# A convolution with max pooling: the GpSimd block of each step regrouped and placed behind the sums of the next step

## Chip, cores, metric

The kernel runs on one core of one Trainium2 chip. The metric is the device time of one execution in microseconds (us); the kernel before was run 13 times, and the median counts.

## What is computed

A 3x3 convolution (stride 1, padding 1, no bias) of 16 images with 64 channels of 64x64 points to 128 channels, and then the maximum over 2x2 points. All inputs and outputs are fp32.

```python
x_pad = np.pad(x, ((0, 0), (0, 0), (pad, pad), (pad, pad)), mode='constant')
conv[b, co] += weight[co, ci, kh, kw] * x_pad[b, ci, kh:kh+h, kw:kw+w]
...
output[b, c, i, j] = np.max(conv[b, c, i*pool_size:(i+1)*pool_size,
                                      j*pool_size:(j+1)*pool_size])
```

## The kernel before

**Tiling.** Two images of 64 channels fill the 128 partitions, so the 16 images are 8 pairs. Each pair is cut into 4 parts of 8 output rows (16 image rows). The 32 parts are worked through in 16 steps, i = 0 to 15, i = 4j + q. Step i does part q of two pairs: an even one, called "k" (tile kx, loaded as bf16), and an odd one, called "w" (tile wx, loaded as fp32).

**Fewer products.** The convolution's two rows under one output row share work. Call the four image rows concerned x(-1), x0, x1, x2, and the filter's rows g0, g1, g2. For "k", PA forms (g2 - g1) x1 + g0 x(-1) in one accumulator, PB forms (g0 - g1) x0 + g2 x2 in a second. The row maximum is taken (MX), and g1 (x0 + x1), which both rows have in common, is added to the result afterwards (PR). For "w", P2 forms half of (g0 + g2 - g1) times x1 - x0 in one accumulator, ScalarE writes its negative to a second (SE); P0 adds g0 (x(-1) - x1) to the first and P3 adds g2 (x2 - x0) to the second; after the maximum (mx), P1 adds half of (g0 + g1 + g2) times x0 + x1. PA and PB have 12 matmuls each, the other five have 6 each: 54 matmuls in a step.

**Row operations.** The sums and differences of image rows are made ahead of the matmuls, each as one `tensor_tensor` over 128x512 elements (`row_op`, line 244):

| name in the order | tile | what | engine | read by |
|---|---|---|---|---|
| KS | ks | x0 + x1 of "k" | VectorE | PR |
| WS | ws | x0 + x1 of "w" | VectorE | P1 |
| E | we | x1 - x0 of "w" | VectorE up to step 4, GpSimd from step 5 | P2 |
| Z | wz | x(-1) - x1 of "w" | GpSimd | P0 |
| Y | wy | x2 - x0 of "w" | GpSimd | P3 |

**The rest of a step.** ScalarE copies one accumulator to SBUF (EV, ev), VectorE takes the row maximum with the other (MX, mx: `rowmax`, line 297), ScalarE copies the odd columns (OD, od), and VectorE takes the column maximum of the even columns with them (CM, cm: `colmax`, line 313). That result goes to tile o and is stored by SyncE's queue. There are four accumulators and four o buffers; CM and cm give an accumulator back, and need an o buffer whose store has landed.

**Loads.** `wload` brings the part of the "w" pair for step i + 4 and is issued by SyncE behind the store of CM.i. `kload` brings half of the next "k" pair; GpSimd issues it inside `wy` (line 269), after the Y of the parts q = 1 and q = 2.

**Order.** The order on every engine is written out by hand (`tc.manual_schedule()`): HEAD for steps 0 to 3, STEADY for steps 4 to 12 ("Z+1" in step i means Z of step i + 1), TAIL for the rest. Each engine takes its own steps out of this list in order. Apart from the waits for data there is one that the kernel adds: each GpSimd row operation waits for the last VectorE row operation written ahead of it in the list. `on_vector` (line 74) notes it, `on_gpsimd` (line 78) adds the wait:

```python
def on_gpsimd(inst):
    behind(inst, sbuf_op[0])
    return inst
```

In STEADY, E+1, Z+1 and Y+1 are written in the first half of step i, so the last VectorE row operation ahead of them is WS.i, at the end of step i - 1.

Of the kernel before, what the change touches and what calls it, by code (L numbers as in the profile page):

```python
# [11 lines left out]
def kernel(  # L12
# [265 lines left out]
    ev, od, ot = {}, {}, {}  # L278
# [91 lines left out]
    for m in BLOCKS:  # L370
# [6 lines left out]
        P0.0 P3.0 Z.1 Y.1 OD.0 CM.0 P2.1 ev.0 PB.1 SE.1 mx.0 P0.1 P1.0 MX.1 P3.1 ev.1 od.0 PR.1  # L377
        WS.2 KS.2 E.2 Z.2 Y.2 OD.1 cm.0 CM.1 PA.2 EV.2 P2.2 PB.2 SE.2 mx.1 P1.1 P0.2 MX.2 P3.2
        od.1 ev.2 cm.1 E.3 KS.3 WS.3 Z.3 Y.3 PR.2 PA.3 OD.2 CM.2 P2.3 mx.2 EV.3 PB.3 SE.3 P1.2
        MX.3 P0.3 od.2 P3.3 cm.2 ev.3 PR.3 E.4 KS.4 WS.4 Z.4 Y.4  # L380
    """
    STEADY = """
        PA+0 OD-1 E+1 CM-1 P2+0 mx-1 EV+0 Z+1 PB+0 SE+0 Y+1 P1-1 MX+0 P0+0 od-1 P3+0 cm-1 ev+0
        PR+0 KS+1 WS+1
    """
    TAIL = """
        PA.13 OD.12 CM.12 Y.14 P2.13 mx.12 EV.13 PB.13 SE.13 P1.12 KS.14 MX.13 E.14 P0.13 od.12
        P3.13 cm.12 ev.13 KS.15 PR.13 WS.14 OD.13 PA.14 EV.14 CM.13 mx.13 P2.14 SE.14 PB.14
        MX.14 P1.13 od.13 cm.13 Z.14 P0.14 ev.14 E.15 WS.15 PR.14 OD.14 CM.14 PA.15 P2.15 P3.14
        mx.14 Y.15 Z.15 EV.15.0 EV.15.1 PB.15 MX.15.1 MX.15.0 SE.15 P0.15 P3.15 ev.15.0 mx.15.0  # L390
        ev.15.1 mx.15.1 P1.14 od.14 cm.14 PR.15 OD.15 CM.15 P1.15 od.15 cm.15
    """
    FIRST, LAST = 4, 12
# [53 lines left out]
```

## Time and profile before

| | |
|---|---|
| median of 13 executions | 108.91 us |
| lowest and highest | 108.51 and 110.9 us |
| the profiled execution's own time | 110.9 us |
| its span | 109.1 us |
| TensorE busy | 99.9 us, 900 matmuls |
| VectorE busy | 84.6 us |
| ScalarE busy | 72.9 us |
| GpSimd busy | 60.1 us |
| Z, Y and E on GpSimd | 16, 16 and 11 instructions, mean 1271, 1281 and 1272 ns |
| KS and WS on VectorE | 16 and 16 instructions, mean 468 and 841 ns |
| kx loads by GpSimd's queue | 7, about 0.5 MB written each, 5.9 to 10.5 us to landing |

The profile is of one execution, and its span is what the engines' records cover; the difference of 1.8 us to the execution's time lies around it. A line of the timeline gives the start and the duration in us, the engine, the line in the kernel, the tile written and the tiles read with their shapes, and how often; a bracket gives the engine's idle time before it and what ended it. Line 248 is that of all row operations, so the tile's name tells which one it is. Line 183 is that of all matmuls of the convolution. A matmul's end is modelled, so the length of a group of matmuls is best taken from the start of one group to the start of the next.

### The profile page before, as it was taken

Reading aid. Unit: us, or ns where it says so; the run is one execution under the profiler, and the core shown is the slowest. Engines: PE = TensorE matmul, PEld = TensorE weight load, DVE = VectorE, ACT = ScalarE, POOL = GpSimd, SP = SyncE. Lnnn points to the kernel's source line nnn. Section 1 sums busy time; section 2 is a strip of 40 time slices with the busy share of each in tenths; the row PEclk is TensorE's granted clock in tenths of the full one; section 3 lists DMA queues with packets and bytes.
Section 4 is the critical chain, followed back from the end, with each engine's and each line's share of the span. In section 5 each row is a group of like instructions: output and inputs, shape, how many; then the busy total and the mean of one; then the engine's idle time right before and its main releaser. Section 6 shows DMA issues by size and latency. Waiting matters only on the chain.

```text
span 109.1 us, 2346 instructions
## 1 busy us (share of the span) xinstructions
PE 99.9 (92%) x900; PEld 50.1 (46%) x900; DVE 84.6 (77%) x113; ACT 72.9 (67%) x92; POOL 60.1 (55%) x69
## 2 busy tenths in 40 slices
PE   5999989999999969999999999959999999999820
PEld 2564434444444435555555555525555555545400
DVE  0498989879797989688787868639787888685950
ACT  4568965776867656776867676764867676776820
POOL 6205673915439997948578594904967444535000
PEclk9999999999999999999999999999999999999998
DMA  3999966999978469999948789996939422223052
GB/s 95 325 338 346 262 169 151 204 292 257 297 278 205 176 62 199 296 203 392 262 160 225 107 169 244 224 304 249 265 137 207 165 102 99 96 96 102 0 192 97
DMA packets 12475, 21.96 MB, mean 201 GB/s; under 512 B 944, under 2 KB 9136, under 8 KB 12464
## 3 DMA queue, kind: packets, MB, share of 16 engines
q1 hardware_dynamic: 11312, 18.03, 50.3%
q0 software_dynamic: 1008, 3.65, 21.5%
q8 instruction: 7, 0.11, 0.4%
q10 hardware_dynamic: 144, 0.13, 0.3%
q14 instruction: 4, 0.03, 0.1%
HBM read 17.07 MB, written 8.39 MB: 233 GB/s over the span
## 4 chain that ended last, share of the span: by engine, by line
PE 61%; DMA 17%; DVE 14%; issue 3%; ACT 2%; DVEq 0%
PE acc L183 59%; DMA out_dram<-o 12%; DVE acc L299 6%; DMA wx<-in_x_dram 5%; DVE ws L248 4%; DVE o L318 2%; PE acc L135 2%; ACT od L304 2%; DVE ks L248 2%; DVE we L248 1%; DVE zeros L112 0%; DVE wt L163 0%; DVEq L299 0%; DVEq L318 0%
## 5 line engine op out<-in xcount | busy, mean ns | idle before, releaser
L183 PEld LDWEIGHTS <-wt 64*128 64x128 bf16 x864 | 46.7, 94 | 49.9 <-issue 4.1
L183 PE MATMUL acc<-kx,wt 64*128 64x504 bf16 (+3 forms) x384 | 46.5, 373 | 2.3 <-DVE o L318 2.3
L299 DVE TENSOR_TENSOR acc<-acc,ev 128x1024 f32<-128x1024 f32 (+1 forms) x34 | 39.5, 1165 | 11.5 <-PE acc L183 10.8
L286 ACT COPY ev<-acc 128x1024 f32<-128x1024 f32 (+1 forms) x34 | 32.5, 963 | 14.0 <-PE acc L183 10.2
L304 ACT COPY od<-acc 128x512 f32<-128x512 f32 x32 | 18.8, 587 | 12.7 <-PE acc L183 12.6
L248 POOL TENSOR_TENSOR wz<-wx 128x512 bf16<-128x512 f32 x16 | 20.3, 1271 | 12.5 <-DVE ws L248 5.7
L318 DVE TENSOR_TENSOR o<-acc,od 128x512 f32<-128x512 f32 x32 | 21.9, 689 | 5.0 <-ACT od L304 3.2
L248 POOL TENSOR_TENSOR wy<-wx 128x512 bf16<-128x512 f32 x16 | 20.5, 1281 | 5.0 <-DVE ws L248 5.0
L248 POOL TENSOR_TENSOR we<-wx 128x512 bf16<-128x512 f32 x11 | 14.0, 1272 | 15.0 <-DVE ws L248 9.1
L295 ACT ACTIVATE acc<-acc 128x1024 f32<-128x1024 f32 x16 | 16.1, 1008 | 1.4 <-PE acc L183 1.0
L183 PE MATMUL acc<-ws,wt 64*128 64x504 bf16 (+1 forms) x96 | 13.2, 377 | 0.4 <-DVE acc L299 0.4
L183 PE MATMUL acc<-we,wt 64*128 64x504 bf16 (+1 forms) x96 | 13.2, 377 | 0.4 <-DVE we L248 0.4
L248 DVE TENSOR_TENSOR ws<-wx 128x512 bf16<-128x512 f32 x16 | 13.4, 841 | 0.0
L183 PE MATMUL acc<-ks,wt 64*128 64x504 bf16 (+1 forms) x96 | 13.2, 377 | 0.1
L183 PE MATMUL acc<-wz,wt 64*128 64x504 bf16 (+1 forms) x96 | 13.2, 377 | 0.0
L183 PE MATMUL acc<-wy,wt 64*128 64x504 bf16 (+1 forms) x96 | 13.2, 377 | 0.0
L248 DVE TENSOR_TENSOR ks<-kx 128x512 bf16<-128x512 bf16 x16 | 7.5, 468 | 0.0
L95 POOL DMA_DIRECT2D kx<-in_x_dram x7 | 4.2, 594 | 4.1 <-DVE we L248 4.1
L135 PE MATMUL acc<-zeros 128*128 128x512 bf16 x8 | 3.6, 631 | 1.2 <-DVE zeros L112 1.2
L248 DVE TENSOR_TENSOR we<-wx 128x512 bf16<-128x512 f32 x5 | 3.4, 684 | 0.4 <-DMA wx<-in_x_dram 0.4
L148 PEld LDWEIGHTS <-wq 128*128 128x128 bf16 x28 | 2.3, 124 | 1.0 <-issue 0.6
L148 PE MATMUL acc<-ident,wq 128*128 128x128 bf16 x28 | 2.6, 264 | 0.0
(26 smaller groups left out, 14.9 us busy)
## 6 DMA issues: line engine op xcount, KB each, us to landing
out_dram<-o SPq DMA_DIRECT2D x31, 256.0 KB, 3.7
wx<-in_x_dram SPq DMA_DIRECT2D x8, 512.0 KB, 6.0
wx<-in_x_dram SPq DMA_DIRECT2D x4, 544.0 KB, 6.9
kx<-in_x_dram POOLq DMA_DIRECT2D x4, 496.0 KB, 8.5
wx<-in_x_dram SPq DMA_DIRECT2D x4, 480.0 KB, 4.8
kx<-in_x_dram POOLq DMA_DIRECT2D x3, 528.0 KB, 7.6
kfirst<-in_x_dram SPq DMA_DIRECT2D x1, 544.0 KB, 4.2
ksecond<-in_x_dram SPq DMA_DIRECT2D x1, 512.0 KB, 6.3
```

Of the source, the lines that this page charges most:

```text
L95: return nc.gpsimd.dma_start(out=kx[j][:, lo:hi, :], in_=rows_of(2 * j, lo, hi))
L135: return nc.tensor.matmul(acc[t][:, h], zeros[:, 0:128], zeros, start=True, stop=True, skip_group_check=True)
L148: nc.tensor.transpose(tp[:, (j - lo) * 128 : (j - lo + 1) * 128], wq[:, j : j + 2, :].rearrange("a b c -> a (b c)"), ident,)
L183: nc.tensor.matmul(dst[:, half, i0:i1, o0:o1], wt[lo : lo + CI, m0 + kw - half, :], rows(lo, i0, i1, c0, c1), start=start and kw == 1, sto ...
L248: return engine.tensor_tensor(out=row_out(name, i), in0=row_in(t, f + a, pad), in1=row_in(t, f + b, pad), op=op)
L286: nc.scalar.copy(out=ev[g][:, halves(h)], in_=acc[ta[g]][:, halves(h)])
L295: nc.scalar.mul(acc[t], acc[ta["w", i]], -1.0)
L299: nc.vector.tensor_tensor(out=t, in0=t, in1=ev[g][:, halves(h)], op=MAX)
L304: nc.scalar.copy(out=od[g][:, halves(h)], in_=acc[tb[g]][:, halves(h), :, 1::2])
L318: nc.vector.tensor_tensor(out=o, in0=acc[tb[g]][:, s, :, 0::2], in1=od[g][:, s], op=MAX)
```

## The change

The three GpSimd row operations of a step stay three, but the group is put together differently and written elsewhere in the list. Before, it is E, Z, Y of step i + 1, spread over the first half of step i. After, it is Z and Y of step i + 1 and E of step i + 2, written at the end of step i, behind KS+1 and WS+1. With `on_gpsimd` unchanged, its wait is for WS of step i + 1. E.5 is added at the end of HEAD to start this off. In TAIL, where the order before differs from step to step, the same grouping is written out, and KS.14 and KS.15 are moved next to WS.14 and WS.15. Nothing else is edited.

```diff
-        MX.3 P0.3 od.2 P3.3 cm.2 ev.3 PR.3 E.4 KS.4 WS.4 Z.4 Y.4
+        MX.3 P0.3 od.2 P3.3 cm.2 ev.3 PR.3 E.4 KS.4 WS.4 Z.4 Y.4 E.5
     """
     STEADY = """
-        PA+0 OD-1 E+1 CM-1 P2+0 mx-1 EV+0 Z+1 PB+0 SE+0 Y+1 P1-1 MX+0 P0+0 od-1 P3+0 cm-1 ev+0
-        PR+0 KS+1 WS+1
+        PA+0 OD-1 CM-1 P2+0 mx-1 EV+0 PB+0 SE+0 P1-1 MX+0 P0+0 od-1 P3+0 cm-1 ev+0 PR+0 KS+1
+        WS+1 Z+1 Y+1 E+2
     """
     TAIL = """
-        PA.13 OD.12 CM.12 Y.14 P2.13 mx.12 EV.13 PB.13 SE.13 P1.12 KS.14 MX.13 E.14 P0.13 od.12
-        P3.13 cm.12 ev.13 KS.15 PR.13 WS.14 OD.13 PA.14 EV.14 CM.13 mx.13 P2.14 SE.14 PB.14
-        MX.14 P1.13 od.13 cm.13 Z.14 P0.14 ev.14 E.15 WS.15 PR.14 OD.14 CM.14 PA.15 P2.15 P3.14
-        mx.14 Y.15 Z.15 EV.15.0 EV.15.1 PB.15 MX.15.1 MX.15.0 SE.15 P0.15 P3.15 ev.15.0 mx.15.0
+        PA.13 OD.12 CM.12 P2.13 mx.12 EV.13 PB.13 SE.13 P1.12 MX.13 P0.13 od.12 P3.13 cm.12
+        ev.13 PR.13 KS.14 WS.14 Z.14 Y.14 E.15 OD.13 PA.14 EV.14 CM.13 mx.13 P2.14 SE.14 PB.14
+        MX.14 P1.13 od.13 cm.13 P0.14 ev.14 PR.14 KS.15 WS.15 Z.15 Y.15 OD.14 CM.14 PA.15 P2.15
+        P3.14 mx.14 EV.15.0 EV.15.1 PB.15 MX.15.1 MX.15.0 SE.15 P0.15 P3.15 ev.15.0 mx.15.0
         ev.15.1 mx.15.1 P1.14 od.14 cm.14 PR.15 OD.15 CM.15 P1.15 od.15 cm.15
```

## The prediction

> **What bounds the kernel now.** First the page's busy shares: TensorE (PE) is busy for 92% of the span, VectorE (DVE) 77%, GpSimd (POOL) 55%. So GpSimd's own work is not the limit; it matters only where it makes PE stop.
>
> ```profile
> PE 99.9 (92%) x900; PEld 50.1 (46%) x900; DVE 84.6 (77%) x113; ACT 72.9 (67%) x92; POOL 60.1 (55%) x69
> ```
>
> Then the list of waits, for what stops PE inside the loop. There is one entry of size: two waits for a column maximum (line 318, CM) that frees an accumulator.
>
> ```profile
> PE acc L183 <- DVE o L318: 2.3, 2, 1.3
> ```
>
> Cutting the span at the starts of PA shows which steps hold these two. Columns: stretch, length, then busy time of PE, PEld, DVE, ACT, POOL, clock, DMA share, GB/s.
>
> ```profile
> 36.22:43.17 6.95, 6.00 (x57) 2.96 (x55) 6.47 (x8) 4.21 (x5) 6.63 (x7) 1.00 0.66 124
> 43.17:49.00 5.83, 5.83 (x56) 3.06 (x54) 4.66 (x7) 4.21 (x5) 3.73 (x3) 1.00 1.05 255
> 66.35:73.69 7.34, 6.01 (x56) 3.04 (x53) 4.32 (x6) 4.79 (x6) 3.72 (x3) 1.00 1.00 260
> ```
>
> A step takes 5.83 us with PE filled. Step 5 (begun at 36.22) takes 1.12 us more, step 10 (begun at 66.35) 1.51 us more. In step 5 DVE is busy for 6.47 us with 8 instructions, against 4.66 us with 7. The timeline of step 5 shows why:
>
> ```profile
> 35.10 0.69 DVE L318 TENSOR_TENSOR o<-acc,od 128x512 f32<-128x512 f32 x1
> 35.39 1.28 POOL L248 TENSOR_TENSOR wz<-wx 128x512 bf16<-128x512 f32 x1
> 35.71 1.24 DVE L248 TENSOR_TENSOR ks<-kx 128x512 bf16<-128x512 bf16 x1
> 36.62 1.46 POOL L248 TENSOR_TENSOR wy<-wx 128x512 bf16<-128x512 f32 x1
> 36.87 1.76 DVE L248 TENSOR_TENSOR ws<-wx 128x512 bf16<-128x512 f32 x1
> 38.55 0.68 DVE L318 TENSOR_TENSOR o<-acc,od 128x512 f32<-128x512 f32 x1
> 39.28 1.47 PE L183 MATMUL acc<-kx,wt 64*128 64x512 bf16 x12 [0.95 <-DVE o L318]
> ```
>
> KS.5 takes 1.24 us beside Z.5 where it takes 0.42 elsewhere; WS.5 takes 1.76 us beside Y.5 instead of 0.69. CM.4 behind them comes late, and PB.5 stands waiting for CM.4's accumulator. GpSimd ran into the sums because Z.5, Y.5 have a wait only for WS.4, and that step's group began late: behind Z.4 and Y.4, which themselves waited for WS.4 (31.57). Later steps don't collide; step 7 as the sample:
>
> ```profile
> 48.83 0.69 DVE L248 TENSOR_TENSOR ws<-wx 128x512 bf16<-128x512 f32 x1
> 49.65 1.28 POOL L248 TENSOR_TENSOR we<-wx 128x512 bf16<-128x512 f32 x1 [2.15 <-DVE ws L248]
> 49.84 0.69 DVE L318 TENSOR_TENSOR o<-acc,od 128x512 f32<-128x512 f32 x1 [0.32 <-ACT od L304]
> 50.88 1.28 POOL L248 TENSOR_TENSOR wz<-wx 128x512 bf16<-128x512 f32 x1
> 52.11 1.28 POOL L248 TENSOR_TENSOR wy<-wx 128x512 bf16<-128x512 f32 x1
> 52.81 0.83 PE L183 MATMUL acc<-wz,wt 64*128 64x512 bf16 x6
> 53.46 0.83 PE L183 MATMUL acc<-wy,wt 64*128 64x512 bf16 x6
> ```
>
> Here the group of three (E.8, Z.8, Y.8) starts when WS.7 is done and ends at 53.39, before KS.8 at 54.25. Z.8 and Y.8 are read only at 58.57 and 59.22: a whole step of lead.
>
> The excess of step 10 is another matter: CM.9 (the "w" one) found its output buffer still being stored. The store issued at 60.12 took 12.7 us to land; the median store takes 3.7.
>
> ```profile
> 72.95 0.69 DVE L318 TENSOR_TENSOR o<-acc,od 128x512 f32<-128x512 f32 x1 [1.85 <-DMA out_dram<-o]
> DMA to landing us min/median/max: 12.7/12.7/12.7
> ```
>
> **What the Trainium skill says.** "SBUF — State Buffer", section "Who interferes with whom": a VectorE instruction with two SBUF inputs contends with a GpSimd instruction that reads SBUF, and whichever comes second blocks until the first is through. The trace agrees: KS.5 ends 0.3 us after Z.5 does (36.95 against 36.67), its own 0.42 us coming after the block. The row and column maxima have one input in PSUM; the same section says that a single SBUF input doesn't contend, and mx.6, begun at 50.44 beside E.8 and Z.8, keeps its 1.22 us. "DMA: Bandwidth & Descriptors", section "Queues, rings and completion order": each DMA engine takes turns, packet by packet, between the queues that have work. That fits the slow stores, which were in flight with two kx loads (landing in 10.5 us each).
>
> **The change, part by part.**
>
> *Instructions.* None is added or removed. The order built from the changed kernel is the same on PE, ACT and SP; on DVE only KS.14 and KS.15 move; on POOL the group becomes Z, Y, E. So the change is in waits: Z.i, Y.i wait for WS.i instead of WS.i-1, and E.i+1 comes behind them; E's own wait for WS is dropped, since Z's stands ahead of it.
>
> *The collision of step 5 goes.* E.5 stays where it is (34.16 to 35.44, right behind Y.4), and ends 0.27 us before KS.5 starts at 35.71. Z.5 now waits. KS.5 takes 0.42, the next instruction starting 0.34 after it (24.80 to 25.13 in step 2): WS.5 runs 36.05 to 36.74. Blocked time removed: (1.24 - 0.42) + (1.76 - 0.69) = 1.89 us of DVE. Not all of it is on the path. CM.4 needs OD.4, which ends at 37.02, so it starts at 37.05, not 36.66, and ends at 37.74. Then PB.5 is late no more: P2.5 starts at 37.52 and a group of six matmuls takes 0.65 (44.46 to 45.11), so PB.5 starts at 38.17, with CM.4 done 0.43 before. PE gains 39.28 - 38.17 = **1.11 us**; the step table gives 6.95 - 5.83 = 1.12. This is on the path to the end: PE runs without a gap from there to step 10.
>
> *What is late next in step 5: Z.5 and Y.5.* WS.5 ends 36.74; GpSimd starts 0.13 after it (49.52 to 49.65); two starts are 1.23 apart. Z.5 ends at 38.14, Y.5 at 39.37. P0.5 now comes at 41.22 - 1.11 = 40.11, P3.5 at 40.76. Slack 1.97 and 1.39 us: hidden under PA, P2, PB, P1, cost 0. If the cover were gone, each us of lateness beyond it would cost a us in each of eleven steps.
>
> *The later steps.* Take GpSimd's start from the row named we, which becomes wz, and so on. In step 7, Z.7 runs 49.65 to 50.93 and P0.7 starts 52.81 (slack 1.9); Y.7 ends at 52.16, P3.7 starts 53.46 (slack 1.3); E.8 ends at 53.39, P2.8 starts 55.97 (2.6). The worst step is 11, where everything stood behind the late store: WS.11 ends 74.58, Y.11 would end at 77.2 and P3.11 starts at 78.15, slack 0.9. No step waits: 0.
>
> *The kx loads* are issued inside wy (lines 269 to 275) and go with Y: four of seven (j = 2 and 3) come a step later, less the 1.23 us that Y now comes earlier in its group, e.g. 59.02 becomes 63.6, before the 1.11 shift. On POOL's queue E now stands behind them: Z 1.23, Y 1.23, load 0.70, E 1.27, so step 9's E.10 ends at 61.12 + 4.43 = 65.55, and KS.10 starts at 65.84: 0.29 us to spare, on the old clock for both. If that were overrun, DVE has the 0.32 us it idles before CM and the 0.43 above, 0.75 in all, before PE waits. Cost 0. Their data are wanted later still: j = 3's first half is read by KS.12 at 78.94 against a landing near 63.6 + 10.5 = 74.1; in hand 4.8 us. What the shifted transfers do to stores and wx loads isn't shown by the trace. Bounds: -1.5 us if step 10's store wait vanishes, +1.5 if one such wait is added (that step's excess). I take 0: the bytes and the number of overlapping steps are the same. wx loads themselves keep their place on SP's queue, and E, now behind Z and Y, asks for them 2.5 us later.
>
> *The tail.* KS.14 leaves its place before MX.13, where DVE stood idle for 0.53 anyway. KS.15 now goes ahead of WS.15: WS.15 moves from 96.37 to 96.71, the next start 0.61 later is 97.32, exactly where CM.14 starts now. Z.15 then ends at 97.39 + 0.13 + 1.27 = 98.79 and Y.15 at 100.0; P0.15 starts at 100.31, P3.15 at 100.96. Slack 1.5 and 1.0: cost 0. Z.14, Y.14, E.15 end by 95.4; P0.14 at 94.92 needs only Z.14 (92.9).
>
> **Sum.** The profiled execution took 110.9 us (span 109.1 and 1.8 around it): 110.9 - 1.1 = 109.8, if its store wait stays. It is the highest of the 13 times. The median, 108.91, is lower by about as much as that wait of 1.5 us and some more, so I take the median run to be without most of it, and the collision, which follows from the fixed order, to be in every run: 108.9 - 1.1 = **107.8 us**.
>
> **Rivals.**
> - *The late store returns in typical runs* (slower). Place: a CM behind the moved kx loads, j = 2 or 3. With four output buffers, a store may take 71.10 - 60.12 = 11.0 us (from its issue to the CM four later, where it would start undisturbed) before DVE stops. For: the four stores issued from 60.12 to 68 took 8.4 to 12.7 us beside two kx loads, and PE now gives DMA 1.1 us less. Against: the loads of 38.02 and 42.40 left the stores issued from 42 to 47 at 8.1 at most, 2.9 under the limit. One such wait: 107.8 + 1.5 = 109.3; both bursts: 110.8.
> - *Another wait takes the place of the removed one*: Z and Y, now a step later, or E behind a load running into KS. Against: slacks of 0.9 to 1.9 us and the 0.29 + 0.75 us. To eat the whole gain Y.5 would have to come 2.5 us late, or a tenth of a us be lost in eleven steps beyond all slack: 108.9.
> - *The store wait gets rarer*: the loads start 1.2 us earlier in a step, farther ahead of the next stores. Then runs that had some of it lose it too: 107.3.
>
> **Chances.** A measurement of this kernel can tell about 0.3% (0.33 us) from no change. Forecast 107.8: 0.75; rarer store wait: 0.07; another wait in its place: 0.08; late store: 0.10. So faster 0.82, same 0.08, slower 0.10. The range goes from 107.1 (a little below the third rival) to 108.9, taking in the second and leaving out the first.
>
> **What would show it.** Step 5 as long as its neighbours (5.8 us); KS and WS nowhere over 0.7 us after the head (WS.1 at 11.18, 2.11 us, stays, as the head doesn't change there); no wait of P0 or P3 for GpSimd; GpSimd's idle time ahead of wz, not we. Wrong would be: PE waiting for POOL in each step, or CM waiting for a store in most runs, or step 5 still long with KS.5 short.

## The result, and the profile after

| | before | after |
|---|---|---|
| median | 109.0 us (48 runs) | 107.75 us (11 runs) |
| lowest to highest | 108.37 to 110.9 us | 107.32 to 108.19 us |
| the profiled execution | 110.9 us, span 109.1 | 107.48 us, span 105.7 |

The ratio after to before is 0.9874, with a 95% interval of 0.9848 to 0.9900: the change makes the kernel 1.1 to 1.7 us faster (1.25 by the medians). Forecast were 107.8 us and a gain of 1.1. The profiled execution before is the slowest of its 48; the wait of its step 5 is there in a profile of 108.88 us too (`before_six_o`, below), that of its step 10 is not.

The page's busy shares after: PE is at 94% (92 before), its busy time all but the same (99.9 before), in a shorter span.

```profile
PE 99.0 (94%) x900; PEld 45.7 (43%) x900; DVE 82.6 (78%) x113; ACT 72.8 (69%) x92; POOL 60.2 (57%) x69
```

In the list of waits, PE's entry for the column maximum (2.3 us in two waits) is gone. What tops the list now is GpSimd waiting for WS ahead of each group; that idle time costs nothing, since GpSimd is not the bottleneck. The second line is VectorE's short idling before the column maximum, which the prediction counted as cover (time that a delay may eat before PE waits) and which is still there.

```profile
POOL wz L248 <- DVE ws L248: 23.3, 12, 3.6
DVE o L318 <- ACT od L304: 3.6, 11, 0.3
```

The span cut at the starts of PA, steps 5, 6 and 10 (columns as before). Step 5 takes 5.83 us like its neighbour, step 10 takes 5.84, and PE is busy in all of it.

```profile
35.42:41.25 5.83, 5.83 (x56) 2.64 (x54) 4.66 (x7) 4.21 (x5) 4.31 (x4) 1.00 0.71 177
41.25:47.09 5.84, 5.84 (x57) 2.64 (x55) 4.67 (x7) 4.21 (x5) 4.31 (x4) 1.00 0.99 242
64.43:70.27 5.84, 5.84 (x57) 2.64 (x55) 4.67 (x7) 4.21 (x5) 4.31 (x4) 1.00 1.01 265
```

Step 5 in the timeline, with the same instructions as the prediction shows of before, and those that follow them:

```profile
34.90 0.41 DVE L248 TENSOR_TENSOR ks<-kx 128x512 bf16<-128x512 bf16 x1
35.24 0.69 DVE L248 TENSOR_TENSOR ws<-wx 128x512 bf16<-128x512 f32 x1
36.00 1.27 POOL L248 TENSOR_TENSOR wz<-wx 128x512 bf16<-128x512 f32 x1 [1.37 <-DVE ws L248]
36.24 0.69 DVE L318 TENSOR_TENSOR o<-acc,od 128x512 f32<-128x512 f32 x1 [0.32 <-ACT od L304]
37.24 1.27 POOL L248 TENSOR_TENSOR wy<-wx 128x512 bf16<-128x512 f32 x1
37.36 1.46 PE L183 MATMUL acc<-kx,wt 64*128 64x512 bf16 x12
38.45 0.58 POOL L95 DMA_DIRECT2D kx<-in_x_dram x1
39.04 1.29 POOL L248 TENSOR_TENSOR we<-wx 128x512 bf16<-128x512 f32 x1
39.31 0.81 PE L183 MATMUL acc<-wz,wt 64*128 64x512 bf16 x6
39.96 0.81 PE L183 MATMUL acc<-wy,wt 64*128 64x512 bf16 x6
```

KS.5 and WS.5 take 0.41 and 0.69 us with GpSimd at rest. CM.4 starts as soon as OD.4 is there, and PB.5 starts 1.94 us after PA.5 (35.42 to 37.36) without a wait; before it was 3.06. Z.5 ends 2.0 us before P0.5, Y.5 1.45 before P3.5, and E.6 is done (40.33) 0.41 before KS.6 (40.74).

The two spans differ by 3.4 us, more than the medians. The starts of PA split that: 0.80 us lie ahead of PA.5 (36.22 to 35.42), in the head that the change doesn't touch; 1.12 in step 5; 1.50 in step 10, where the profiled execution before had its late store. The first is no gain: over the thirteen profiles of this study PA.5 starts anywhere from 35.35 to 36.73. The third isn't one either, as `before_six_o` shows below. The stores of after land in time; the line gives the lowest, median and longest time from issue to landing.

```profile
DMA to landing us min/median/max: 2.1/3.6/8.1
```

### The profile page after: what moved, and what is told of

Its sections match the earlier page's. It is cut to its first block, busy times and chain, and to the rows that moved or that the text cites. A ratio compares the mean times of both kernels' runs of the same rounds, so it can differ in the third digit from the quotient of the medians.

```text
span 105.7 us, 2338 instructions
## 1 busy us (share of the span) xinstructions
PE 99.0 (94%) x900; PEld 45.7 (43%) x900; DVE 82.6 (78%) x113; ACT 72.8 (69%) x92; POOL 60.2 (57%) x69
## 4 chain that ended last, share of the span: by engine, by line
PE 82%; DVE 6%; DMA 6%; ACT 1%; issue 1%; SPq 0%; DVEq 0%
PE acc L183 81%; DMA ksecond<-in_x_dram 6%; DVE acc L299 5%; PE acc L135 2%; DVE o L318 1%; ACT kx L344 1%; ACT od L304 1%; SPq L100 0%; DVE zeros L112 0%; DVEq L299 0%
## 5 line engine op out<-in xcount | busy, mean ns | idle before, releaser
L183 PEld LDWEIGHTS <-wt 64*128 64x128 bf16 x864 | 42.9, 94 | 50.9 <-issue 1.6
L286 ACT COPY ev<-acc 128x1024 f32<-128x1024 f32 (+1 forms) x34 | 32.5, 963 | 12.6 <-PE acc L183 11.0
L248 DVE TENSOR_TENSOR ws<-wx 128x512 bf16<-128x512 f32 x16 | 12.0, 751 | 0.1
L248 DVE TENSOR_TENSOR ks<-kx 128x512 bf16<-128x512 bf16 x16 | 6.7, 416 | 0.0
L350 DVE TENSOR_TENSOR wq<-wraw 128x192 bf16<-128x192 f32 x1 | 0.5, 502 | 2.4 <-DMA wraw<-in_weight_dram 2.4
L135 PEld LDWEIGHTS <-zeros 128*128 128x128 bf16 x8 | 1.0, 140 | 2.8 <-issue 1.7
```

The source lines that it names most:

```text
L135: return nc.tensor.matmul(acc[t][:, h], zeros[:, 0:128], zeros, start=True, stop=True, skip_group_check=True)
L183: nc.tensor.matmul(dst[:, half, i0:i1, o0:o1], wt[lo : lo + CI, m0 + kw - half, :], rows(lo, i0, i1, c0, c1), start=start and kw == 1, sto ...
L248: return engine.tensor_tensor(out=row_out(name, i), in0=row_in(t, f + a, pad), in1=row_in(t, f + b, pad), op=op)
L286: nc.scalar.copy(out=ev[g][:, halves(h)], in_=acc[ta[g]][:, halves(h)])
L350: "D2": lambda: on_vector(nc.vector.tensor_sub(out=slots(D2), in0=g2, in1=g1)),
```

## The experiments

Each run is compared with the kernel before on the same chip. The regrouped kernel's own ratio is 0.9874 (0.9848 to 0.9900).

### The collision alone

**collision_back** puts the one collision back into the regrouped kernel.

```diff
-        ... E.4 KS.4 WS.4 Z.4 Y.4 E.5
+        ... E.4 KS.4 WS.4 Z.4 Y.4 E.5 Z.5 Y.5
...
         for s in STEADY.split():
+            if i == 4 and s in ("Z+1", "Y+1"):
+                continue
             steps[s[:-2]](i + int(s[-2:]))
```

> The regrouped kernel with the one collision put back: Z.5 and Y.5 are written ahead of KS.5 and WS.5 again, so they start right behind E.5; all other groups, waits and the tail stay as after. If the collision of step 5 is where the gain comes from (my theory), KS.5 and WS.5 take about 1.2 and 1.8 us, step 5 about 6.9 us, and the time is 107.75 + 1.1 = 108.9 us (ratio to before 0.998 to 1.001). If the gain comes from the regrouping of all steps or from the later kx loads (rival), it stays near 107.8 us (ratio 0.987 to 0.99).

Measured: 108.96 us, ratio 1.0004 (0.9976 to 1.0032). The whole gain is gone. Its step 5, cut at the starts of PA and then as a timeline:

```profile
35.87:42.79 6.92, 5.98 (x56) 2.96 (x54) 6.44 (x8) 4.21 (x5) 3.62 (x4) 1.00 0.68 125
```

```profile
35.03 1.27 POOL L248 TENSOR_TENSOR wz<-wx 128x512 bf16<-128x512 f32 x1
35.35 1.23 DVE L248 TENSOR_TENSOR ks<-kx 128x512 bf16<-128x512 bf16 x1
36.26 1.46 POOL L248 TENSOR_TENSOR wy<-wx 128x512 bf16<-128x512 f32 x1
36.51 1.75 DVE L248 TENSOR_TENSOR ws<-wx 128x512 bf16<-128x512 f32 x1
38.92 1.47 PE L183 MATMUL acc<-kx,wt 64*128 64x512 bf16 x12 [0.94 <-DVE o L318]
```

These are the lines of before to within a few hundredths: 6.92 us for the step, 0.94 us of waiting for CM.4. The regrouping of the other steps, kept here, brings nothing by itself that the interval (0.3 us either way) would show.

**collision_one_input** asks what in the sums collides. The collision stays, but KS.5 and WS.5 are made by an instruction with a single SBUF input, and KS.8, beside which GpSimd is idle, too.

```diff
+        src = t[:, f : f + 2 * R, :].rearrange("p (r two) w -> p r w two", two=2)
...
+            return nc.vector.tensor_reduce(
+                out=row_out(name, i), in_=src, axis=mybir.AxisListType.X, op=ADD
+            )
```

> collision_back (Z.5 and Y.5 ahead of KS.5 and WS.5), but KS.5 and WS.5 are made by a tensor_reduce over the pairs of rows, which has one input in SBUF; KS.8, which no GpSimd instruction overlaps, is made so too, as a measure. If two SBUF inputs are what makes the sums block behind Z.5 and Y.5, KS.5 takes as long as KS.8 (about 1.1 us for 1024 elements), Z.5 and Y.5 keep 1.27 us, and step 5 loses only what the reduces are longer: 2 x 1.1 = 2.2 us against 1.1 for the plain sums, 1.1 more, of which 0.75 is covered: about 0.35, so 108.1 us. Rival, that any VectorE instruction on SBUF is slowed beside GpSimd: KS.5 and WS.5 take over 1.8 us each, 109 us or more.

Measured: 108.42 us, ratio 0.9941 (0.9920 to 0.9961).

```profile
35.32 1.21 DVE L258 TENSOR_REDUCE ks<-kx 128x512 bf16<-128x1024 bf16 x1
36.44 1.23 DVE L258 TENSOR_REDUCE ws<-wx 128x512 bf16<-128x1024 f32 x1
...
53.30 1.21 DVE L258 TENSOR_REDUCE ks<-kx 128x512 bf16<-128x1024 bf16 x1
```

```profile
35.00 1.27 POOL L248 TENSOR_TENSOR wz<-wx 128x512 bf16<-128x512 f32 x1
36.24 1.27 POOL L248 TENSOR_TENSOR wy<-wx 128x512 bf16<-128x512 f32 x1
```

KS.5 takes 1.21 us right across Z.5, as does KS.8 with no neighbour, and Y.5 keeps its 1.27 us where it took 1.46. So GpSimd doesn't slow every VectorE instruction that reads SBUF. The reduce differs from the sum in more than its inputs, but the column maximum is a `tensor_tensor` like the sums, with one input in PSUM, and CM.4 of after keeps its 0.69 us in the middle of Z.5 (lines above). Both agree with the Trainium skill's page "SBUF — State Buffer" (section "Who interferes with whom"): two SBUF inputs on VectorE are what block, and it names tensor_reduce as an instruction that never contends on this chip. The time came out 0.3 us over what I expected. In the profile the two reduces put the next instruction off by 1.12 and 1.15 us, 2.27 in all against 0.95 for the plain sums. Less the 0.75 of cover that leaves 0.57, and PB.5 starts 2.51 us after PA.5, 0.57 late. The reduce of KS.8 costs step 8 another 0.09 (5.85 us against 5.76), so 107.75 becomes 108.4. I had put the excess of step 5 at 1.1 instead of 1.32, and that of KS.8 at nothing.

### Loads, stores and tail

**loads_at_old_place** takes back the later kx loads.

```diff
             on_gpsimd(row_op(nc.gpsimd, "we", i, 1, 0, SUB))
+            j, q = divmod(i, NQ)
+            if q == 1 and j + 1 < NP // 2:
+                kload(j + 1, 0, H // 2 + 1)
+            if q == 2 and j + 1 < NP // 2:
+                kload(j + 1, H // 2 + 1, H)
...
-        if q == 1 and j + 1 < NP // 2:
+        if i == 1 and j + 1 < NP // 2:
...
-        if q == 2 and j + 1 < NP // 2:
+        if i == 2 and j + 1 < NP // 2:
```

> The regrouped kernel, but the four kx loads of j = 2 and 3 are issued behind the E of the group instead of behind Y one step later: the same instant in the same step as in the kernel before. My theory: the place of the loads is worth nothing, 107.75 us within 0.3 (ratio 0.985 to 0.99), no step longer than 5.9 us. Rival, that the later loads are what keeps the stores on time: a column maximum waits for a store again in some runs, 108.2 to 109.3 us.

Measured: 107.52 us, ratio 0.9862 (0.9824 to 0.9899): no difference to the regrouped kernel that shows (the interval is 0.4 us either way). The last two loads are issued 1.4 and 1.6 us ahead of PA, as in the kernel before (1.5 and 1.6), the first two 2.6 and 0.8 us earlier than there. So the later place of the loads is worth nothing that can be seen here.

**before_six_o** takes the store waits away from the kernel before, **after_six_o** from the regrouped one.

```diff
-    o_pool = ctx.enter_context(tc.tile_pool(name="o_pool", bufs=4))
+    o_pool = ctx.enter_context(tc.tile_pool(name="o_pool", bufs=6))
```

> The kernel before with six o buffers instead of four, so that a store may take about 22 us before a column maximum waits for it (6 buffers: 3 steps, 17 us). Only the store waits are taken away; the collision of step 5 stays. My theory: typical runs had few of them, so 108.7 to 109.0 us (0 to 0.3 faster), with a smaller spread and none above 109.8. Rival, that the gain of the change is mostly store waits that went: 107.8 to 108.2 us.

> The regrouped kernel with six o buffers instead of four. My theory: no column maximum waits for a store in it as it is (longest landing in its profile 8.1 us of 11.0 allowed), so nothing changes: 107.75 us within 0.3. Rival, that some runs still lose time to stores: 107.3 to 107.5 us.

Measured: before_six_o 108.93 us, ratio 1.0007 (0.9977 to 1.0038); after_six_o 107.62 us, ratio 0.9873 (0.9833 to 0.9912). Nothing is gained in either. (Six buffers are three steps, about 17 us; the 22 us in the expectation is wrong.) The profile of before_six_o is of an execution of 108.88 us. It has no wait for a store, and the wait of step 5 is as before:

```profile
38.77 1.47 PE L183 MATMUL acc<-kx,wt 64*128 64x512 bf16 x12 [0.95 <-DVE o L318]
```

Step 5 takes 6.95 us in it and 5.84 in after_six_o; every other step from 2 to 14 is as long in the one as in the other, to 0.02 us. So the profiles show no second place where the change gains or loses.

The spread of before_six_o (108.48 to 110.24) isn't smaller: I was wrong that the upper runs come from stores alone. No other profile of this study has a column maximum waiting for a store, as step 10 of before had. Between the profiles it is the start that differs: from E.0 to PA.5 it is 27.6 to 27.8 us in all thirteen, and E.0 starts anywhere from 7.65 to 9.02 us. In the two latest, before (8.50) and old_tail (9.02), E.0 waits 0.41 and 1.26 us for its wx load. Whether that is also what spreads the runs that have no profile isn't shown.

**old_tail** has the tail of before under the regrouped loop.

```diff
-        PA.13 OD.12 CM.12 P2.13 mx.12 EV.13 PB.13 SE.13 P1.12 MX.13 P0.13 od.12 P3.13 cm.12
-        ev.13 PR.13 KS.14 WS.14 Z.14 Y.14 E.15 OD.13 PA.14 EV.14 CM.13 mx.13 P2.14 SE.14 PB.14
...
+        PA.13 OD.12 CM.12 Y.14 P2.13 mx.12 EV.13 PB.13 SE.13 P1.12 KS.14 MX.13 P0.13 od.12
+        P3.13 cm.12 ev.13 KS.15 PR.13 WS.14 OD.13 PA.14 EV.14 CM.13 mx.13 P2.14 SE.14 PB.14
...
```

> The regrouped steps with the tail of the kernel before (its order of KS.14, KS.15, Y.14, Z.14, E.15, Y.15, Z.15; only E.14, already done, is taken out). My theory: the tail's new order costs and brings nothing, 107.75 us within 0.3 (ratio 0.985 to 0.99). Rival: part of the gain beyond 1.1 us is the tail's, 108.0 to 108.2 us.

Measured: 107.89 us, ratio 0.9903 (0.9877 to 0.9928). The interval overlaps that of the regrouped kernel, so the times alone leave some tenths of a us open. The profiles close it: from PA.13 to the last P1 it is 18.27 us here (83.09 to 101.36) and 18.26 after (81.78 to 100.04). The profiled execution itself took 1.33 us longer (108.81), of which 1.31 lie ahead of PA.5. In this tail a sum does run into the group (KS.14 takes 0.80 us beside Y.14), and PE doesn't notice.

### How much room Z and Y have

**e_first** uses up the slack: the group in the order E, Z, Y.

```diff
-        WS+1 Z+1 Y+1 E+2
+        WS+1 E+2 Z+1 Y+1
```

> The regrouped kernel with the group in the order E, Z, Y instead of Z, Y, E, in the loop alone. Y is then done 1.23 us later, which leaves about 0.06 us of the slack of 1.3 us before P3, and Z 0.67 of 1.9. My theory (the slacks as worked out): no change, 107.75 us within 0.3, at most a few hundredths of a us of waiting in a step. Rival, that the slack is smaller than it looks (a wait that the profile hides): each of nine steps loses, over 108.5 us.

Measured: 109.62 us, ratio 1.0037 (1.0003 to 1.0071): slower than the kernel before. My expectation failed by 1.9 us, and the rival's number came true. But the profile doesn't show the rival's reason. In steps 5, 6 and 7 there is no wait for GpSimd; P3.5 starts 0.22 us after Y.5 is done (40.02, 40.24). Step 8 loses 0.8 us (6.60 against 5.76):

```profile
52.95 0.68 DVE L248 TENSOR_TENSOR ws<-wx 128x512 bf16<-128x512 f32 x1
...
54.66 1.28 POOL L248 TENSOR_TENSOR we<-wx 128x512 bf16<-128x512 f32 x1 [2.91 <-DVE o L318]
...
57.11 1.28 POOL L248 TENSOR_TENSOR wy<-wx 128x512 bf16<-128x512 f32 x1
```

```profile
58.44 0.82 PE L183 MATMUL acc<-wy,wt 64*128 64x512 bf16 x6 [0.41 <-POOL wy L248]
```

GpSimd starts E.9 not 0.1 us after WS.8 but 1.03. The bracket names a column maximum of VectorE, but E reads nothing of it: E waits for WS.8 (done at 53.63) and for the wx load of step 9. That load was issued at 43.55, beside a kx load, and the trace gives its landing:

```profile
DMA to landing us min/median/max: 11.0/11.0/11.0
```

43.55 + 11.0 = 54.55, and E starts at 54.66. So E, whose result PE wants only in the next step, holds up Z and Y, which PE is about to want, when its load is late. The profile is of one of the two fastest of the 14 executions (108.70); the median lies 0.9 us higher, and no profile shows which waits make up the rest. The place of E behind Z and Y is a part of the change that I had seen (E asks for its load 2.5 us later) and given no value.

**e_first_wx_early** tests this: the order E, Z, Y again, with the wx loads from step 5 on issued one step earlier. **after_wx_early** has the same loads with the group as in the change.

```diff
-        if g[0] == "k" and g[1] + NQ < N and h is None:
-            wload(g[1] + NQ)
+        if g[0] == "k" and h is None:
+            if g[1] == 0:
+                wload(NQ)
+            if g[1] + NQ + 1 < N:
+                wload(g[1] + NQ + 1)
```

> The group in the order E, Z, Y as in e_first, and every wx load from step 5 on issued one step earlier on SyncE's queue (behind the store of CM.i comes the load for step i + 5 instead of i + 4). New theory for e_first: not the slack of Z and Y failed, but E, now first, asks for its wx load 2.46 us sooner (10.3 us after its issue, where one took 11.0), and Z and Y stand behind it. Then a load that has a step more brings e_first back to 107.75 us within 0.3. Rival, that the slack of Z and Y is short in most runs whatever the loads do: 109 us or more stay.

> The regrouped kernel with every wx load from step 5 on issued one step earlier. Theory: with E last in the group its load is asked for after 12.7 us at the soonest, and none took longer (9.2 at most in its profile), so nothing waits for wx loads and nothing is gained: 107.6 to 107.8 us. Rival, that loads still cost time in typical runs: 107.3 us or less. A loss (over 108.0) would mean that the earlier loads get in the way of kx loads and stores.

Measured: e_first_wx_early 107.79 us, ratio 0.9878 (0.9833 to 0.9923); after_wx_early 107.49 us, ratio 0.9859 (0.9809 to 0.9908). With a step more for the load, the order E, Z, Y costs nothing in the time, though Y's slack is as short as in e_first (0.23 us in step 5) and one load took 11.8 us. So the loss of e_first comes with the load's lateness; the short slack alone doesn't make it. With E last there is nothing for earlier loads to bring; 107.49 is the lowest median of the study but for no measurable reason.

**e_twice_first** goes past the slack: E is computed twice ahead of Z and Y.

```diff
-        WS+1 Z+1 Y+1 E+2
+        WS+1 E+2 E+2 Z+1 Y+1
```

> The regrouped kernel with E computed twice ahead of Z and Y (E, E, Z, Y in the loop; the second E writes the same rows again), so the group starts Z 2.46 us later. My theory: Z comes 0.57 us and Y 1.15 us after PE wants them, PE waits for GpSimd in each of the nine steps that the loop serves, 9 x 1.15 = 10.4 us, about 118 us (116 to 119.5). Rival, that GpSimd's lateness is absorbed by the slack of other engines: under 112 us.

Measured: 114.1 us, ratio 1.046 (1.041 to 1.051). PE does wait for GpSimd, but the cost is 6.4 us over the regrouped kernel, not 10.4. The starts of PA tell how: the steps from step 5 on take 7.02, 6.04, 6.87, 6.03, 6.74, 6.12 us, in turn 0.9 to 1.2 and 0.2 to 0.3 us longer than after, 6.2 us in the nine steps.

```profile
41.67 0.82 PE L183 MATMUL acc<-wy,wt 64*128 64x512 bf16 x6 [0.41 <-POOL wy L248]
41.82 0.68 DVE L248 TENSOR_TENSOR ws<-wx 128x512 bf16<-128x512 f32 x1
...
42.96 1.48 PE L183 MATMUL acc<-kx,wt 64*128 64x512 bf16 x12
```

In step 5 the waits come at P0 and P3, after the matmuls of P1 on which od, cm and so KS.6 and WS.6 depend. These go on while PE stands still: WS.6 ends at 42.50, 0.46 us ahead of PA.6, where it otherwise ends 0.5 us behind PA. The next group gets a start of about 1 us, and its step pays only the rest. I had taken WS's place against PA as fixed.

### The other collision

**head_e_first** eases the block in the head, where WS.1 stands behind Z.0 and Y.0.

```diff
-        KS.0 E.0 WS.0 PB.0 EV.0 X1 Z.0 Y.0 VGP P2.0 MX.0 SE.0 X2 PA.1 EV.1 WS.1 KS.1 E.1 PR.0
+        KS.0 E.0 WS.0 PB.0 EV.0 X1 Z.0 Y.0 VGP P2.0 MX.0 SE.0 X2 PA.1 EV.1 E.1 KS.1 WS.1 PR.0
```

> The regrouped kernel with the other collision eased: in the head, E.1 KS.1 WS.1 instead of WS.1 KS.1 E.1, so that E.1, for which P2.1 waits, isn't the third behind a blocked WS.1. My theory (a blocked sum costs what is queued behind it on VectorE): P2.1 starts about 0.5 us earlier, 107.2 us (107.0 to 107.5). Rival, that the head is bound by the first loads and by ScalarE's copies, so nothing is gained or Z.1, now behind WS.1, comes late: 107.75 to 108.1 us.

Measured: 107.78 us, ratio 0.9893 (0.9869 to 0.9917): nothing is gained. The block moves from WS.1 to E.1 (first line; the second is P2.1):

```profile
11.02 1.74 DVE L248 TENSOR_TENSOR we<-wx 128x512 bf16<-128x512 f32 x1
...
13.49 0.82 PE L183 MATMUL acc<-we,wt 64*128 64x512 bf16 x6
```

P2.1 no longer waits: it starts 0.65 us, the length of a group, after P3.0 (12.84 to 13.49). But in the regrouped kernel's profile its wait was only 0.08 us (12.75 to 13.48); the 0.59 that I worked from (13.05 to 14.29) is that of the profiled execution before, where the head ran later. In return PB.1 starts 0.86 us after P2.1, 0.21 late.

## Why the prediction was right

- **What bounds the kernel, and the collision of step 5.** Right. Put back alone, it takes back the whole gain; the block goes with the two SBUF inputs. One reading is off: KS.5 ends 0.28 us after Z.5, which is less than its own 0.42 us, so by these spans not all of that came after the block.
- **Its worth of 1.11 us.** Right: step 5 went from 6.95 to 5.83 us. The 1.89 us of blocked VectorE less 0.32 and 0.43 of cover give 1.14, and the same rule gives the 0.57 us of collision_one_input. The times agree less closely: 1.11 lies at the lower edge of the ratio's interval of 1.1 to 1.7 us, the medians differ by 1.25, and collision_back lies 1.21 above after. The profiles have no second place for the rest, while the starts of before_six_o and after_six_o differ by 0.22 us; that the median met the forecast to 0.05 us is in part luck.
- **The slacks of Z, Y and E at no cost.** Right in all steps of after (list of waits: no PE wait for GpSimd). The numbers held: for step 5, 1.97 and 1.39 us were predicted, 2.04 and 1.45 measured. E ended 0.41 us ahead of KS.6 instead of 0.29 as worked out for a step with a load, since the load takes 0.59 us of GpSimd, not the 0.70 that I took.
- **The kx loads, 0.** Right by loads_at_old_place and after_six_o. Their shift was worked out as 4.6 us; against PA it is 1.2, 3.8, 4.5 and 4.6 us, as the collision had held up the first two in the kernel before.
- **The tail, 0.** Right to 0.01 us in the profiles.
- **The late store.** I took the median run to be without most of it: right. As an explanation of the spread of before it isn't borne out, and both rivals built on stores fell.
- **What the prediction undervalued.** That E comes behind Z and Y was counted as 2.5 us more for its load and as worth nothing. Without it, with the same collision removed, the kernel is slower than before (e_first, 109.62). It brings no gain over before, where Z and Y had a step of lead and a late E held up nobody; with the loads issued when they are, it is what lets Z and Y do without that lead.

## What to carry to other kernels

When two engines block each other, look for the step where one of them catches up: here five GpSimd instructions in a row ran into the only two VectorE instructions of a step that block, and one such meeting cost 1.1 us, while eight steps with the same work had none. Tie the second engine's group to the end of the first's blocking instructions, and work out for each member the time between its result and its reader. In the group, put last whatever waits for a transfer and isn't needed soon: an instruction's place in a queue decides whose slack a late load eats.

## What the runs showed of the hardware

- The block works in both directions: KS.5 of before waited for Z.5, and Y.5 then took 1.46 us instead of 1.27 beside the tail of KS.5.
- A blocked sum ends sooner after the GpSimd instruction ahead of it than its own time would have it: KS.5 of before 0.28 us (own time 0.42), WS.5 0.55 us (own time 0.69); collision_back has 0.28 and 0.54. GpSimd's spans are rough, so it isn't shown whether a part of the sum runs ahead of the block.
- A tensor_reduce over pairs, 1024 elements in and 512 out, takes 1.21 us for bf16 and 1.23 for fp32 input; the tensor_tensor sum takes 0.41 for bf16 and 0.69 for fp32.
- A wx load of about 0.5 MB, 5.3 to 6.0 us in the median of a profile, took 11.0 us beside a kx load in e_first, up to 11.8 in e_first_wx_early and up to 12.6 in before; a store of 0.25 MB took 12.7 instead of 3.7 in one execution.
